# First norm of a decoder step: conditioning weights by quarters, 1/rms spread without a copy, last product's chunks in another order

## The chip, the cores and the metric

The kernel runs on one core of a Trainium2 chip. The metric is the device time of one execution in microseconds; below, "us" is always that. The engines are named as in the profile: PE (TensorE matmul), PEld (its weight loads), DVE (VectorE), ACT (ScalarE), POOL (GpSimd), SP (SyncE, which issues most DMAs).

## The reference, cut to what matters

One layer of a decoder works on 1024 prompt rows and 8 x 8 sample rows, 1088 rows of 1024 features. The prompt and each of the 8 sample sequences have a conditioning vector of their own, so there are 9 sets of shift and scale.

```
def rms_norm(x, g):
    y = xf * lax.rsqrt(jnp.mean(xf * xf, axis=-1, keepdims=True) + NORM_EPS)
    return y * g
def ada_mod(c, w, b):
    m = jax.nn.silu(c) @ w + b
    shift, scale, gate = jnp.split(m, 3, axis=-1)
...
h = rms_norm(x, norm_mix) * (1 + sc) + sh
P = h @ w_in                      # 1024 x 4352, in 34 blocks of 128 columns
... RWKV-7 branch, pooling branch, merge, w_out, residual
h = rms_norm(x, norm_mlp) * (1 + sc) + sh
x = x + gt * (square(relu(h @ w_ff1)) @ w_ff2)
y = rms_norm(x, norm_final)
```

## The kernel before, in words

Features lie on the 128 partitions and the 1088 rows along the free dimension, so x is eight tiles of 128x1088 (index kb). All large products are done in three passes with split operands: a value is split into hi (rounded) and lo (the rest), and each product is hi*hi + hi*lo + lo*hi (`mm3`, three matmuls). One row kb of h therefore becomes two tiles, `self.hh[kb]` and `self.hl[kb]`; in the profile both are called hx, and their numbers tell them apart (hx_147 and hx_148 are hi and lo of kb 0, hx_149 and hx_150 of kb 1, up to hx_161 and hx_162 of kb 7). A block of w_in is loaded in two halves of four kb each (`weights`, L157: a DMA to wraw, an ACT rounding to whi at L167, a DVE or POOL subtraction to wlo at L168). An output block has three chunks of columns (CH: 364, 362, 362), so one kb of one block takes 9 matmuls.

**Order of the work.** On DVE, ACT, POOL and SP a scheduler of the framework sets the order of the instructions; on PE the order is that in which the code emits them. `Pace` (L80) decides it: a counter `pace.t` adds an estimated time for each matmul, `back` is the stream of large products, and a `fore` generator yields the time to wait before its next step is put between them.

**The start** (`start`, L341, called in `phase1`). The eight x tiles are loaded by SP, squared on ACT (L361) and summed on DVE (L365). `smp` is the sample part of x, loaded once more in its own layout by a DMA on ACT's queue (L349). `stats` sums over the partitions with nine matmuls into po. `rms` (L281) takes the square root on ACT, the reciprocal on DVE (rt, 128x9), copies it to 128 columns for each of the nine blocks (R, L289), transposes these on PE (L155) so that 1/rms lies along the rows on all partitions, and copies the result from PSUM to rb on ACT (L302).

Shift and scale are made by `ada_part` (L239). w_ada_mix lies in thirds of 1024 columns, of which part 0 holds shift and scale of kb 0 to 3 and part 1 those of kb 4 to 7; eight DMAs of 512 KB load a part (aw, L371). A round of four small matmuls (32x512, wc<-aw,sT) multiplies two kb; four rounds make a part. ACT copies the sum to asb (L255), four matmuls with the table sel turn it into columns (L260; these are called the vector products below), DVE adds the bias (am, L263) and makes g = (1 + scale) * norm (L268). Then for each kb DVE makes h = x*g*rb (L390), ACT hi = round(h + shift) (L392), DVE lo = h + shift - hi (L394), and the 64 sample columns go by smp (L385 to L387, L393, L395).

The first two blocks of w_in, J4 and J12, are taken kb by kb in turn (`order` in `phase1`): 18 matmuls for each kb, 144 in all, and then the other 32 blocks of the stream, block by block. Part 0 of the conditioning stands before all of them, part 1 in the midst: `part(1, (0, 0, 3000, 1500), 1500)`.

**The end** (`phase2`: `last`, L1380, and `norm3`, L1401). The last group of the w_ff2 product goes by three chunks of columns, FCH = (0, 448), (448, 384), (832, 256); for each of the eight blocks m DVE adds the product to x (L1433; the 64 sample columns, which are the last ones, take an extra DVE step at L1436 and an addition on POOL, L1438), ACT squares it (L1410), DVE sums the squares (L1412), PE makes the stats, `rms` gives rb, and DVE multiplies (L1423; in the last chunk two blocks go by POOL and ACT, L1420 and L1421) before SP stores o_y (L1424). `rms` is also called in `norm2` (L1278), the norm before the second half of the layer.

Of the kernel before, what the change touches and what calls it, by code (L numbers as in the profile page):

```python
# [18 lines left out]
P = 128  # L19
# [98 lines left out]
class K:  # L118
# [162 lines left out]
    def rms(self, po, col, blocks, out, pool):  # L281
# [6 lines left out]
        R = self.row(pool, "R", 1, w=9 * 128).rearrange("p (b j) -> p b j", j=128)  # L288
        nc.vector.tensor_copy(R[:, :k, :], r.unsqueeze(2).to_broadcast([P, k, 128]))  # L289
        yield 2000  # L290
        for i in range(0, k, 4):
            m = min(4, k - i)
            ps = self.ps("wc")
            for j in range(m):
                self.tr(ps[:, j * 128:(j + 1) * 128], R[:, i + j, :], self.kc("ident"))
# [45 lines left out]
    def start(self, st, order):  # L341
# [4 lines left out]
        aw = lambda: st.tile([P, 1024], F32, tag="aw", bufs=8, name=self.nm("aw"))  # L346
        asb = st.tile([P, 512], F32, name="asb")
        smp = st.tile([P, 8, 64], F32, name="smp")
        nc.scalar.dma_start(smp, io["xT"][:, :, NPR:NT].rearrange("k p n -> p k n"))  # L349
# [6 lines left out]
        for kb in range(8):  # L356
            x = self.row(st, "x", 8)
            nc.sync.dma_start(x, io["xT"][kb])
            xs.append(x)
            sq = self.row(st, "sq", 3)  # L360
            nc.scalar.activation(sq, x, AF.Square)  # L361
            if t is None:
                t = sq
            else:
                nc.vector.tensor_tensor(t, t, sq, op=ALU.add)  # L365
        ws = []

        def load(i):
            for k in range(8):
                ws.append(aw())  # L370
                nc.sync.dma_start(ws[-1], io["w_ada_mix"][k, i])  # L371
# [3 lines left out]
        self.stats(po, t, blocks, True, True)  # L375
        rb = self.row(st, "rb", 1)
        pr, sa = slice(0, NPR), slice(NPR, NT)

        def part(i, gaps, turn):
            yield from self.ada_part("w_ada_mix", i, lambda: ws.pop(0), asb, self.am, "b_mix", (4 * i, 8 + 4 * i), gaps, turn)  # L380
            self.mod_scale(g, self.am, "norm_mix", 4 * i, 4 * i + 4)
            ks = slice(4 * i, 4 * i + 4)
            seq = lambda t: t[:, ks, 1:9].unsqueeze(3).to_broadcast([P, 4, 8, 8])
            s4 = smp[:, ks].rearrange("p k (q t) -> p k q t", t=TS)
            nc.vector.tensor_tensor(smp[:, ks], smp[:, ks], rb[:, sa].unsqueeze(1).to_broadcast([P, 4, 64]), op=ALU.mult)  # L385
            nc.vector.tensor_tensor(s4, s4, seq(g), op=ALU.mult)
            nc.vector.tensor_tensor(s4, s4, seq(self.am), op=ALU.add)  # L387
# [1169 lines left out]
```

## Time and profile before

| | us |
|---|---|
| three runs: median (lowest to highest) | 1761.83 (1758.38 to 1764.14) |
| the profiled execution, its own time | 1760.32 |
| its span in the trace | 1758.5 |
| PE busy in the span | 1688.9 (96%) |
| DVE busy / ACT busy / POOL busy | 846.8 / 546.0 / 242.9 |
| HBM read and written | 138.64 MB and 38.84 MB |

The profiled execution took 1.8 us more than its span, and 1.5 us less than the median. A row of a timeline gives the start in us from the span's start, the time until the end, the engine, the line, what is written and read, how many instructions of the kind are merged, and in brackets how long the engine had been idle and what ended that.

### The profile page before, as it was taken

What the parts mean: (1) busy time and instruction counts of PE and PEld (TensorE: products, weight loads), DVE (VectorE), ACT (ScalarE), POOL (GpSimd) and SP (SyncE); (2) the same over time, 40 slices, a digit from 0 to 9 for tenths busy, and PEclk for the clock granted to TensorE, in tenths of its full rate; (3) what the DMA queues carried; (4) which work ended last, traced back from release to release, by engine and by line L of the source; (5) the groups of instructions that cost most, each with busy time, mean ns of one, the idle gap of its engine ahead of it and who ended that gap; (6) DMA issues with size and microseconds to landing.
All of it is one profiled execution on the core that took longest, in us unless ns stands there. A gap on an engine that the chain in (4) does not pass through costs nothing.

```text
span 1758.5 us, 32538 instructions
## 1 busy us (share of the span) xinstructions
PE 1688.9 (96%) x13705; PEld 1582.7 (90%) x13705; DVE 846.8 (48%) x1546; ACT 546.0 (31%) x1100; POOL 242.9 (14%) x315
## 2 busy tenths in 40 slices
PE   5999999999999999998999999999999999999997
PEld 2989879887887898897889999999999999999996
DVE  5577475646663654344436643333333343323356
ACT  4443343334333433221224521213121222212132
POOL 0110111000000000003313511111111111111111
PEclk9999999999999999998999999999999999999999
DMA  8233314232413332849742211111111111111112
GB/s 336 83 126 119 124 65 138 83 104 88 131 42 127 97 120 72 315 156 356 257 150 78 85 61 42 49 43 43 48 42 48 44 43 48 42 49 43 43 42 103
DMA packets 80084, 179.61 MB, mean 102 GB/s; under 512 B 16481, under 2 KB 23137, under 8 KB 79937
## 3 DMA queue, kind: packets, MB, share of 16 engines
q1 hardware_dynamic: 72128, 156.66, 26.0%
q10 hardware_dynamic: 7664, 20.42, 3.4%
q8 instruction: 108, 1.77, 0.4%
q0 software_dynamic: 144, 0.44, 0.1%
q14 instruction: 40, 0.32, 0.1%
HBM read 138.64 MB, written 38.84 MB: 101 GB/s over the span
## 4 chain that ended last, share of the span: by engine, by line
PE 86%; DVE 5%; DMA 4%; ACT 2%; issue 1%; SPq 0%; DVEq 0%; ACTq 0%; POOL 0%
PE mm L148 58%; PE w L148 24%; PE wc L148 3%; DMA smp<-in_xT 1%; PE w L155 1%; DMA wt<-d_x 1%; DMA wraw<-in_w_in 1%; DVE wlo L168 1%; DMA d_th<-px 0%; DMA hx<-in_xT 0%; DMA t<-d_th 0%; DVE ma L1305 0%; DMA aw<-in_w_ada_mix 0%; DVE hx L1423 0%; DVE t L1303 0%
## 5 line engine op out<-in xcount | busy, mean ns | idle before, releaser
L148 PE MATMUL mm<-hx,whi 128*128 128x362 f32 (+2 forms) x2608 | 684.6, 344 | 9.0 <-DVE t L1246 6.5
L148 PEld LDWEIGHTS mm<-hx,whi 128*128 128x128 f32 x2608 | 459.0, 192 | 47.6 <-issue 28.4
L148 PE MATMUL mm<-hx,wlo 128*128 128x362 f32 (+3 forms) x1304 | 430.1, 330 | 1.8 <-DVE wlo L168 1.8
L167 ACT ACTIVATE whi<-wraw 128x512 fp32r<-128x512 f32 x246 | 155.0, 630 | 537.4 <-PE w L148 365.3
L148 PE MATMUL mm<-ma,whi 128*128 128x364 f32 (+1 forms) x1280 | 318.8, 330 | 0.0
L148 PEld LDWEIGHTS mm<-hx,wlo 128*128 128x128 f32 x1304 | 250.5, 192 | 2.3 <-DVE wlo L168 2.1
L148 PEld LDWEIGHTS mm<-ma,whi 128*128 128x128 f32 x1280 | 227.0, 189 | 6.7 <-issue 5.0
L168 DVE TENSOR_TENSOR wlo<-wraw,whi 128x512 fp32r<-128x512 f32 x157 | 111.9, 713 | 210.6 <-ACT whi L167 210.0
L148 PE MATMUL mm<-ma,wlo 128*128 128x364 f32 (+1 forms) x640 | 210.7, 329 | 0.0
L168 POOL TENSOR_TENSOR wlo<-wraw,whi 128x512 fp32r<-128x512 f32 x89 | 117.3, 1318 | 666.4 <-ACT whi L167 666.2
L1433 DVE SCALAR_TENSOR_TENSOR hx<-mm,aq,hx 128x364 f32<-128x364 f32 (+4 forms) x136 | 74.7, 587 | 206.4 <-PE mm L148 206.3
L148 PE MATMUL w<-mb,whi 128*128 128x362 f32 x640 | 159.0, 330 | 0.6 <-DVE rs L1436 0.6
L148 PEld LDWEIGHTS mm<-ma,wlo 128*128 128x128 f32 x640 | 120.9, 189 | 0.0
L148 PEld LDWEIGHTS w<-mb,whi 128*128 128x128 f32 x640 | 114.0, 191 | 0.8 <-issue 0.8
L1327 DVE TENSOR_TENSOR ft<-ft 128x362 f32<-128x362 f32 (+1 forms) x96 | 53.0, 576 | 127.4 <-ACT ft L1326 127.0
L148 PE MATMUL w<-mb,wlo 128*128 128x362 f32 x320 | 105.4, 329 | 1.3 <-DVE wlo L168 1.3
L148 PE MATMUL w<-hx,whi 128*128 128x362 f32 x416 | 103.5, 330 | 0.1
L148 PE MATMUL mm<-hid,whi 128*128 128x364 f32 (+4 forms) x304 | 75.3, 330 | 0.0
L148 PEld LDWEIGHTS w<-hx,whi 128*128 128x128 f32 x416 | 73.4, 190 | 1.2 <-issue 0.8
L1326 ACT ACTIVATE ft<-mm 128x364 f32<-128x364 f32 x64 | 29.3, 474 | 128.4 <-PE mm L148 128.3
L148 PE MATMUL w<-hx,wlo 128*128 128x362 f32 x208 | 67.8, 326 | 0.0
L148 PEld LDWEIGHTS w<-mb,wlo 128*128 128x128 f32 x320 | 61.1, 191 | 1.7 <-DVE wlo L168 1.7
(301 smaller groups left out, 2074.5 us busy)
## 6 DMA issues: line engine op xcount, KB each, us to landing
wraw<-in_w_ff SPq DMA_DIRECT2D x134, 256.0 KB, 2.6
wraw<-in_w_in SPq DMA_DIRECT2D x68, 256.0 KB, 3.0
hid<-in_w_ada_mlp SPq DMA_DIRECT2D x24, 512.0 KB, 5.1
d_th<-px SPq DMA_DIRECT2D x22, 544.0 KB, 3.1
wt<-d_x SPq DMA_DIRECT2D x20, 544.0 KB, 4.3
t<-d_th ACTq DMA_DIRECT2D x16, 544.0 KB, 6.7
aw<-in_w_ada_mix SPq DMA_DIRECT2D x16, 512.0 KB, 7.1
wraw<-in_w_out SPq DMA_DIRECT2D x32, 256.0 KB, 2.7
```

The source lines that it names most:

```text
L148: return self.nc.tensor.matmul(out, lhsT, rhs, **kw)
L155: self.nc.tensor.transpose(out, in_, ident)
L167: nc.scalar.activation(hi, raw, AF.Copy)
L168: (nc.gpsimd if n % 2 and n >= self.solo else nc.vector).tensor_tensor(lo, raw, hi.bitcast(F32), op=ALU.subtract)
L1326: nc.scalar.activation(t[:, :n], ps[:, :n], AF.Relu)
L1327: nc.vector.tensor_tensor(t[:, :n], t[:, :n], t[:, :n], op=ALU.mult)
L1433: nc.vector.scalar_tensor_tensor(x[:, c0:c0 + m], ps[:, :m], gt[:, 0:1], x[:, c0:c0 + m], op0=ALU.mult, op1=ALU.add)
```

## The change

**The conditioning by quarters.** w_ada_mix is no longer taken in two parts of 1024 columns but in four quarters (`qi`) of 512: shift and scale of two kb. A quarter is loaded by four DMAs of 512 KB (two tiles of 128x2x4x256, so pieces of 1 KB instead of 4 KB), and takes two rounds of four matmuls and one step of four vector products with 9 columns. The table for these is sel, summed once on POOL from the two halves of the old one. Quarter 0 is done before the large products begin, in a fixed order: round, stats, round, `rms`, asb, vector products, `rows(0)`. Quarters 1 to 3 stand among the products by `rest`: waits of 1000, 4500 and 5000 before a quarter's first round, 500 between its rounds, 1200 before its vector products, and none behind these.

**Two rows of h from each.** `rows(qi)` makes kb 2*qi and 2*qi + 1; for kb 0 and 1 h, hi and lo are made in three pieces, the chunks CH. The sample part is multiplied for two kb at a time.

**smp** is loaded by POOL instead of ACT. The last square and its addition are cut in two, 512 and 576 columns.

**1/rms without a copy.** R is gone: the transposes read rt with a stride of zero, in all calls of `rms`. In the first norm their results go to three tiles of the tag mm; in the last chunk of the kernel the six DVE multiplications read 1/rms from PSUM (`self.rps`).

**The last product.** FCH is turned round: the columns 640 to 1088 come first, with the samples, then 256 to 640, then 0 to 256. In the first chunk all eight m are multiplied in order; in the second m 0 to 3, and m 4 to 7 are written in the code behind the stats of the third.

```
-        R = self.row(pool, "R", 1, w=9 * 128).rearrange("p (b j) -> p b j", j=128)
-        nc.vector.tensor_copy(R[:, :k, :], r.unsqueeze(2).to_broadcast([P, k, 128]))
...
-                self.tr(ps[:, j * 128:(j + 1) * 128], R[:, i + j, :], self.kc("ident"))
+                self.tr(ps[:, j * 128:(j + 1) * 128], r[:, i + j:i + j + 1].to_broadcast([P, 128]), self.kc("ident"))
+            self.rps = ps
+            if out is None:
+                return
...
-        nc.scalar.dma_start(smp, io["xT"][:, :, NPR:NT].rearrange("k p n -> p k n"))
+        nc.gpsimd.dma_start(smp, io["xT"][:, :, NPR:NT].rearrange("k p n -> p k n"))
+        sel = st.tile([P, 9], F32, name="sel4")
+        nc.gpsimd.tensor_tensor(sel, self.kc("sel")[:, 0:9], self.kc("sel")[:, 9:18], op=ALU.add)
...
-        def load(i):
-            for k in range(8):
-                ws.append(aw())
-                nc.sync.dma_start(ws[-1], io["w_ada_mix"][k, i])
+        def load(qi):
+            for r in range(2):
+                w = st.tile([P, 2, 4, 256], F32, tag="aw", bufs=4, name=self.nm("aw"))
+                for s in range(2):
+                    o = s * 512 + qi % 2 * 256
+                    nc.sync.dma_start(w[:, s], io["w_ada_mix"][4 * r:4 * r + 4, qi // 2, :, o:o + 256].rearrange("k p c -> p k c"))
+                ws.append(w)
...
         load(0)
         back = self.stream(None, order)
-        self.stats(po, t, blocks, True, True)
+        load(1)
...
+        def round_(qi, r):
+            if r == 0:
+                ps[qi] = self.ps("wc")
+            w = ws.pop(0)
+            for k in range(4):
+                self.mm(ps[qi][32 * k:32 * k + 32, :], self.sT[:, 4 * r + k, :], w[:, :, k, :], start=r == 0, stop=r == 1, tile_position=(0, 32 * k))
+
+        def vectors(qi, wait):
+            kb = 2 * qi
+            asb = st.tile([P, 512], F32, tag="asb", bufs=1, name=self.nm("asb"))
+            nc.scalar.activation(asb, ps.pop(qi), AF.Copy)
+            yield wait
+            pv = self.ps("wc")
+            for i in range(4):
+                self.mm(pv[:, i * 9:(i + 1) * 9], asb[:, i * 128:(i + 1) * 128], sel, start=True, stop=True)
...
+            self.mod_scale(g, self.am, "norm_mix", kb, kb + 2)
...
+        def head():
+            round_(0, 0)
+            self.stats(po, t, blocks, True, True)
+            round_(0, 1)
+            yield from self.rms(po, 0, blocks, rb, "mm")
...
-        self.pace.run(iter(()), [part(0, (0, 3500, 0, 0), 1000), self.rms(po, 0, blocks, rb, st)])
-        load(1)
+        first()
+        rows(0)
+        load(2)
+        load(3)
...
-            yield from part(1, (0, 0, 3000, 1500), 1500)
+            for qi in range(1, 4):
+                yield (1000, 4500, 5000)[qi - 1]
+                round_(qi, 0)
+                yield 500
+                round_(qi, 1)
+                yield from vectors(qi, 1200)
+                rows(qi)
...
+                if ci == 2:
+                    for o in late:
+                        o()
+                yield from self.rms(po, 0, bl, rb[:, c0:c0 + n])
...
+                if ci < 2:
+                    late = [] if ci == 0 else [lambda m=m, out=out, r=rb[:, c0:c0 + n]: out(m, r) for m in range(4, 8)]
+                    for m in range(8 if ci == 0 else 4):
+                        out(m, rb[:, c0:c0 + n])
+                else:
+                    for m in (7, 6, 0, 1, 2, 3, 4, 5):
+                        out(m, rb[:, c0:c0 + n] if m > 5 else self.rps[:, :n], m > 5)
...
-FCH = [(0, 448), (448, 384), (832, 256)]
+FCH = [(640, 448), (256, 384), (0, 256)]
```

**Where instructions move: PE, the last vector products of the first norm.** Before, the vector products of part 1 (wc_410, from asb) make shift and scale of kb 4 to 7, whose first tile is hx_155; the rows around them are these:

```order
L148 MATMUL mm_373<-hx_149,wlo_243 128x362
L148 MATMUL wc_410<-kct,asb 128x18 x4
L148 MATMUL mm_356<-hx_151,whi_236 128x364
L148 MATMUL mm_356<-hx_152,whi_236 128x364
L148 MATMUL mm_356<-hx_151,wlo_237 128x364
```

Now the vector products of quarter 3 (wc_539, from asb_528) make shift and scale of kb 6 and 7, whose first tiles are hx_159 and hx_160:

```order
L148 MATMUL mm_355<-hx_157,wlo_488 128x362
L148 MATMUL wc_539<-sel_175,asb_528 128x9 x4
L148 MATMUL mm_333<-hx_159,whi_473 128x364
L148 MATMUL mm_333<-hx_160,whi_473 128x364
L148 MATMUL mm_333<-hx_159,wlo_474 128x364
```

Before, 36 matmuls of kb 2 and 3 stood between the vector products and the first matmul on a tile that they lead to; now there are none in quarter 3, 9 in quarter 2 (between wc_449 and hx_155) and 15 in quarter 1 (between wc_374 and hx_151).

**DVE, quarter 2.** Before, in part 1, DVE's rows from the vector products (am from wc_410) to the first lo tile (hx_156) were these:

```order
L263 TENSOR_TENSOR am<-wc_410,part 128x2x36
L268 SCALAR_TENSOR_TENSOR g_172<-am,part 128x36
L386 TENSOR_TENSOR smp<-smp,g_172 128x256
L390 SCALAR_TENSOR_TENSOR h_420<-x_198,g_172,rb_255 128x1024
L390 SCALAR_TENSOR_TENSOR h_426<-x_203,g_172,rb_255 128x1024
L387 TENSOR_TENSOR smp<-smp,am 128x256
L394 SCALAR_TENSOR_TENSOR hx_156<-h_420,am,hx_155 128x1024
```

Now the lo parts of the second half of the weights, wlo_474 and wlo_489, stand among them:

```order
L168 TENSOR_TENSOR wlo_474<-wraw_471,whi_473 128x512
L402 TENSOR_TENSOR am<-wc_449,part 128x2x18
L268 SCALAR_TENSOR_TENSOR g_172<-am,part 128x18
L413 SCALAR_TENSOR_TENSOR h_456<-x_199,g_172,rb_245 128x1024
L416 TENSOR_TENSOR smp<-smp,g_172 128x128
L413 SCALAR_TENSOR_TENSOR h_465<-x_204,g_172,rb_245 128x1024
L168 TENSOR_TENSOR wlo_489<-wraw_486,whi_488 128x512
L417 TENSOR_TENSOR smp<-smp,rb_245 128x128
L419 SCALAR_TENSOR_TENSOR hx_156<-h_456,am,hx_155 128x1024
```

In the other quarters the rows are the same without the two wlo; the kb 2, 4 and 6 have their lo tile behind both h of the quarter.

**ACT, before the square root of the first norm.** rt is the square root (w_176 and w_177 hold the stats), whi the rounded weights of J4 and J12. Before:

```order
L361 ACTIVATE sq_215<-x_213 128x1088
L286 ACT_TABLE_LOAD
L286 ACTIVATE rt_261<-w_176,eps 128x9
L302 ACTIVATE rb_255<-wc_266 128x512
L302 ACTIVATE rb_255<-wc_272 128x512
L167 ACTIVATE whi_236<-wraw_234 128x512
```

Now:

```order
L363 ACTIVATE sq_216<-x_214 128x576
L167 ACTIVATE whi_229<-wraw_227 128x512
L167 ACTIVATE whi_235<-wraw_233 128x512
L286 ACT_TABLE_LOAD
L286 ACTIVATE rt_264<-w_177,eps 128x9
L395 ACTIVATE asb_282<-wc_246 128x512
```

Both whi, which wait for their DMAs, have moved ahead of the table load and the square root; on DVE both wlo stand ahead of the reciprocal in the same way. On SP the two wraw are issued behind four DMAs of w_ada_mix instead of eight.

At the end of the kernel the eight multiplications of the second chunk (128x384) stand on DVE ahead of the last four additions of the third, in both kernels.

64 lines of the change are left out of this document (35 added, 29 removed).

## The prediction

> **What bounds the kernel now.** I read the chain that ended last, then windows by stage, then the timeline of the start and of the end. The chain by engine, three stages of the start, a stretch of the middle:
>
> ```profile
> PE 86%; DVE 5%; DMA 4%; ACT 2%; issue 1%; SPq 0%; DVEq 0%; ACTq 0%; POOL 0%
> 22.60:37.70 15.10, 13.25 (x66) 4.10 (x65) 8.07 (x13) 5.65 (x10) 0.00 (x0) 1.00 1.05 403
> 37.70:53.80 16.10, 16.03 (x100) 13.32 (x98) 12.90 (x19) 6.98 (x15) 0.00 (x0) 1.00 0.26 106
> 53.80:55.90 2.10, 0.27 (x3) 0.01 (x1) 2.10 (x5) 1.07 (x2) 0.00 (x0) 1.00 0.01 4
> 1000.00:1200.00 200.00, 200.00 (x1211) 200.00 (x1211) 75.95 (x137) 46.75 (x92) 34.04 (x37) 1.00 0.16 51
> ```
>
> (The columns of a window: us, then busy us and instructions of PE, PEld, DVE, ACT and POOL, granted clock, DMA share, GB/s.) PE is the bound: in the middle it is never idle, and a large matmul takes 200/1211 = 0.165 us. Whatever PE loses at the start moves all that follows; only the start and the end, where PE waits, can give anything. The start to the first rows of h:
>
> ```profile
> GB/s 0 58 211 410 409 410 411 425 405 401 403 417 421 239 0 237 361 353 291 324 397 415 430 419 417 397 306 348 419 433 415 395 424 419 415 433 401 69 0 0
> SPq L371 <- DMA smp<-in_xT: 10.3, 1, 10.3
> 17.24 1.28 ACT L286 ACT_TABLE_LOAD   x1
> 22.66 0.27 ACT L286 ACTIVATE rt<-w,eps 128x9 f32<-128x9 f32 x1 [4.14 <-PE w L148]
> 23.21 1.35 DVE L289 COPY R<-rt 128x1152 f32<-128x1152 f32 x1
> 24.62 1.12 PE L155 MATMUL wc<-kct,R 128*128 128x128 f32 x4
> 30.26 1.33 ACT L167 ACTIVATE whi<-wraw 128x512 fp32r<-128x512 f32 x2 [2.09 <-DMA wraw<-in_w_in]
> 34.07 2.47 DVE L390 SCALAR_TENSOR_TENSOR h<-x,g,rb 128x1024 f32<-128x1024 f32 x2
> 39.19 0.35 DVE L395 TENSOR_TENSOR hx<-smp,hx 128x64 fp32r<-128x64 f32 x2
> 39.46 0.19 PEld L148 LDWEIGHTS w<-hx,whi 128*128 128x128 f32 x1 [0.37 <-DVE hx L395]
> ```
>
> The DMAs run at about 410 GB/s (40 slices of 45 us) with a hole of 239, 0 and 237, some 2 us, while SP waits for smp before it issues aw. The first h begins at 34.07, and PE has the first block's third chunk, with the samples, at 39.46.
>
> **The change, the start: what comes earlier.** The hole goes, since SP no longer waits for smp (-2 us). wraw stands behind 2.1 MB of aw instead of 4.2: at 410 GB/s -5.1 us, so it lands at 30.26 - 7.1 = 23.2. The DMAs now move pieces of 1 KB; nothing here shows their price, so I take the rate as it is, and add up to 0.8 us in the range. But ACT now does both whi first (1.33: to 24.5), then the table load that was hidden under the stats before (1.28: 25.8), then the root (0.27: 26.1). Against 22.93 the root is 3 us later. Then the reciprocal (0.25 with its gaps), nine transposes of rt at 1.12/4 (2.5; R's 1.35 us are saved here; a source with stride zero costs, I assume, what R's cost), the vector products (0.96, row below) and am and g (0.5): h begins at about 30.3, and at 29 if PE is quicker by half at the transposes.
>
> The steps from there on, each with its row:
>
> ```profile
> 41.46 1.06 PE L148 MATMUL wc<-aw,sT 128*32 128x512 f32 x8
> 46.73 0.96 PE L148 MATMUL wc<-kct,asb 128*128 128x18 f32 x8
> 47.54 0.57 PE L148 MATMUL mm<-hx,whi 128*128 128x364 f32 x2
> 47.73 0.23 DVE L263 TENSOR_TENSOR am<-wc,part 128x72 f32<-128x72 f32 x1 [3.13 <-PE wc L148]
> 48.00 0.20 DVE L268 SCALAR_TENSOR_TENSOR g<-am,part 128x36 f32<-128x36 f32 x1
> 48.23 0.42 DVE L386 TENSOR_TENSOR smp<-smp,g 128x256 f32<-128x256 f32 x1
> 48.57 2.47 DVE L390 SCALAR_TENSOR_TENSOR h<-x,g,rb 128x1024 f32<-128x1024 f32 x2
> 51.29 2.48 DVE L394 SCALAR_TENSOR_TENSOR hx<-h,am,hx 128x1024 fp32r<-128x1024 f32 x2
> 1722.01 4.85 DVE L1423 SCALAR_TENSOR_TENSOR hx<-hx,part,t 128x448 f32<-128x448 f32 x8
> 1740.11 4.33 DVE L1423 SCALAR_TENSOR_TENSOR hx<-hx,part,t 128x384 f32<-128x384 f32 x8
> ```
>
> For kb 0 and 1 DVE works in pieces: from 4.85/8 = 0.61 for 448 columns and 4.33/8 = 0.54 for 384, a piece of 364 takes 0.52 and one of 298 0.45. Its order has six pieces of h (2.98), a smp step (estimated at 0.29 for half of 256 columns), then lo: the first after 3.8 us; five more pieces of lo, two smp steps and the sample columns: another 3.2. So PE has the chunk with the samples at 30.3 + 7.0 = 37.3, against 39.46: 2.2 us earlier.
>
> **What PE then still has to do.** Until the next block begins it has 137 matmuls in both kernels (22.6 us). Before, two rounds and one step of vector products were left; now six rounds and three steps. That is 4 x 1.06 + 2 x 0.81 (46.73 to 47.54) = 5.9 us more, work that before lay in the waits of the first 37 us. Without any stall PE would reach the next block at 37.3 + 22.6 + 6 x 1.06 + 3 x 0.81 + 0.5 of small gaps = 69.2. Before it was there at 69.13 (row below), stalls included (39.5 + 22.6 + 2 x 1.06 + 0.81 + 0.5 and 3.5 for the stall below and the slow clock after it make 69.0): so far nothing is won.
>
> **The stalls that it adds.** From the end of a quarter's vector products to its first lo tile DVE needs, by the rows above, 51.29 + 1.24 - 47.73 = 4.8 us, and 4.5 with smp half as wide. PE needs that lo with its second matmul. As the order in front shows, PE's cover between is 15 matmuls in quarter 1, 9 in quarter 2, none in quarter 3 (36 before, 5.9 us, which is why this stall is not in the trace now).
> - Quarter 1: 4.5 - 16 x 0.165 = 1.9.
> - Quarter 2: wlo_474 stands ahead of am and waits for whi, which waits for PE's last use of the old weights right before the vector products: 0.63 + 0.69 + 0.1 - 0.81 = 0.6 later; wlo_489 adds 0.7. So 5.8 - 10 x 0.165 = 4.1.
> - Quarter 3: 4.5 - 0.165 = 4.3.
> - In each the chunk with the samples waits again: smp, the second lo and hx<-smp stand behind the first lo, 0.29 + 1.24 + 0.2 = 1.7, and PE comes to it after five matmuls, 0.8: 0.9 each, 2.7.
>
> Together 13.0 us. Then the clock. Before, PE has one such stall, and this followed it:
>
> ```profile
> 55.16 1.28 DVE L168 TENSOR_TENSOR wlo<-wraw,whi 128x512 fp32r<-128x512 f32 x2
> 55.90 0.43 PE L148 MATMUL mm<-hx,wlo 128*128 128x364 f32 x1 [1.83 <-DVE wlo L168]
> 57.00:58.00 1.00, 1.00 (x5) 1.00 (x5) 1.00 (x3) 0.33 (x1) 0.00 (x0) 0.50 0.84 256
> 58.00:59.00 1.00, 1.00 (x5) 1.00 (x4) 1.00 (x2) 0.82 (x1) 0.00 (x0) 0.50 0.67 250
> 60.00:61.00 1.00, 1.00 (x6) 1.00 (x6) 0.30 (x1) 0.00 (x0) 0.59 (x1) 0.84 0.09 16
> 61.00:62.00 1.00, 1.00 (x8) 1.00 (x7) 0.00 (x0) 0.00 (x0) 1.00 (x3) 1.00 0.21 62
> 69.13 0.50 PE L148 MATMUL mm<-hx,whi 128*128 128x364 f32 x2
> ```
>
> After 1.83 us of waiting PE ran at half clock for about 3.4 us, which costs 1.7. I take one such spell for each of the three stalls, 5.1, less the 0.8 of each sample wait that slow matmuls cover: +2.7. The Trainium skill ("TensorE: Matmul & The Clock Gate", What's actually happening) has the clock halve after an idle window of about 3.4 us and return after as long a busy one. The trace agrees with the return, but its drop came after 1.83; by the page quarter 1 would keep its clock, and the sum would be 0.9 lower.
>
> So PE begins the next block at 69.2 + 13.0 + 2.7 = 84.9, against 69.13: **+15.8 us**. The old stall of 1.83 and its spell are in the 69.13.
>
> **The middle.** In norm2 and in the first two chunks of the end PE's place for the transposes is fixed and R is ready before it comes there; leaving R out is worth nothing. POOL's sel and smp are hidden: smp is used only after 30 us.
>
> **The end.** The rows of the last chunk:
>
> ```profile
> 1748.07 1.05 PE L148 MATMUL wc<-kct,t 128*128 128x2 f32 x8 [2.87 <-DVE t L1412]
> 1749.65 0.29 DVE L289 COPY R<-rt 128x256 f32<-128x256 f32 x1
> 1750.09 0.66 PE L155 MATMUL wc<-kct,R 128*128 128x128 f32 x2 [0.97 <-DVE R L289]
> 1750.79 0.38 ACT L302 ACTIVATE t<-wc 128x256 f32<-128x256 f32 x1 [1.37 <-PE wc L155]
> 1751.20 3.40 DVE L1423 SCALAR_TENSOR_TENSOR hx<-hx,part,t 128x256 f32<-128x256 f32 x6 [1.26 <-ACT t L302]
> ```
>
> The eight multiplications of 4.33 us still stand ahead of the last additions, so `late` moves nothing. The samples leave the last chunk: four steps rs and a POOL addition go, about 0.4. R goes (0.44 with its gap), and rb on the way to six of the eight multiplications (0.41); the two on POOL and ACT still wait for it, and reading PSUM may cost 0.06 each (0.4). I take **-1.1 us**, from -0.3 to -1.8.
>
> **The sum.** 15.8 - 1.1 = +14.7 us. The profiled execution took 1760.32, so this one would take 1775.0; the median of the runs lies 1.5 above it: **1776.5 us**.
>
> **The rivals.**
> 1. Half the loss: the start gains 2 us more (quick transposes, pieces of 1 KB free) and the clock drops at most once. Then 15.8 - 2 - 3 - 1.1 = +9.7: 1771.5. Against it: three stalls in place of one, two of them twice as long.
> 2. More: the clock stays at half through two spells after each stall, and in the first chunk of kb 0, since PE idles much between 28 and 37. Each further spell costs 1.7, so up to +6: 1782.
> 3. Not slower: the delay is taken back later. Between 69 and 800 PE waits for ACT and DVE in the recurrent branch:
>
> ```profile
> PE w L148 <- ACT wt L577: 5.6, 8, 1.2
> PE w L148 <- DVE wt L1018: 3.7, 3, 2.8
> 200.00:400.00 200.00, 192.42 (x2307) 170.23 (x2308) 116.22 (x221) 75.99 (x168) 15.33 (x31) 0.98 0.28 94
> ```
>
> If these engines ran behind on work of their own, 15 us of head start would let these waits go: without these 9.3 the time is 1767, and with the smaller ones of their kind it falls to 1762 or below. It decides once more than 9 us have vanished. Against it: each of these chains starts from a product that PE itself has just made, and from 200 to 400 DVE is busy for 58% of the time and ACT for 38%, so they follow PE, late as it is.
> 4. SP's hole stays. The Trainium skill ("DMA: Bandwidth & Descriptors", Issuing engines are not separate DMA queues) says that another issuing engine saves only the sequencer's time. The waits row above is a wait for a semaphore, which does go; if it stayed, wraw would land 2 us later: 1778.5, within the range.
>
> **How the numbers follow.** Forecast 0.70, rival 1 0.10, rival 2 0.10, rival 3 0.06, rival 4 0.04. The range reaches from rival 1, less the uncertain end and the shares of the stalls (1768), to rival 2 (1783). A measurement of this kernel tells about 0.3%, 5.3 us, from no change. Rival 3 gives 0.06: half of it faster (0.03), the other within 0.3%, where I put 0.02 of rival 1's lower tail too (0.05). The rest is slower (0.92).
>
> **What would show it.** In the profile of the changed kernel: the root of the first norm at 26 instead of 22.7, behind two whi; h from about 30; then PE waiting for DVE's lo tiles three times, near 2, 4 and 4.5 us, right behind the vector products, with a clock of 0.5 after them; the next block's first matmul near 85 instead of 69; the end some 1 us shorter from PE's last product. If that block begins by 72, or if PE's waits between 85 and 815 are more than 9 us smaller than before, I am wrong.

## The result, and the profile after

The changed kernel takes 1786.97 us (median of 4 runs, 1783.54 to 1788.89), the kernel before 1762.99 beside it (4 runs, 1758.38 to 1771.96): a ratio of 1.0123, 95% interval 1.0100 to 1.0147 (the quotient of the two medians is 1.0136, inside it). It is slower, as forecast, but by 24 us where 14.7 were forecast, and outside the range. The profiled execution took 1786.41 us, with a span of 1784.6; that is 26.1 more than before's span. Medians here are of fast executions: one of 5703.76 us of the kernel before (experiments 9 to 11) and one of 6937.32 us in the eighth experiment are left out.

The start of the changed kernel, from the timelines of PE, ACT and DVE in order of time: the conditioning round, the stats, the second round, the transposes and the vector products on PE; both whi, the table load and the root on ACT; the first piece of h on DVE; and the first block's third chunk.

```profile
19.25 1.94 PE L148 MATMUL wc<-aw,sT 128*32 128x512 f32 x8 [19.25 <-DMA aw<-in_w_ada_mix]
21.12 4.00 PE L148 MATMUL w<-kct,sq 128*128 128x9 f32 x18
25.05 1.93 PE L148 MATMUL wc<-aw,sT 128*32 128x512 f32 x8
26.91 2.18 PE L155 MATMUL mm<-kct,rt 128*128 128x128 f32 x9
28.89 1.72 PE L148 MATMUL wc<-sel,asb 128*128 128x9 f32 x8
...
22.82 1.34 ACT L167 ACTIVATE whi<-wraw 128x512 fp32r<-128x512 f32 x2 [5.42 <-DMA wraw<-in_w_in]
24.17 1.28 ACT L286 ACT_TABLE_LOAD   x1
25.46 0.27 ACT L286 ACTIVATE rt<-w,eps 128x9 f32<-128x9 f32 x1
...
31.16 1.54 DVE L413 SCALAR_TENSOR_TENSOR h<-x,g,rb 128x364 f32<-128x364 f32 x3
...
38.01 0.97 PE L148 MATMUL w<-hx,whi 128*128 128x362 f32 x2 [1.21 <-ACT hx L420]
```

The weights, the root and h come within 0.9 us of the forecast (the weights on time although the DMAs moved 355 GB/s from 15 to 27 us, where the forecast took 410). But the five PE rows join without a gap: PE is busy from 19.25 to 30.6, and all of it at half speed, since a round of 1.94 takes 1.06 later on.

The next rows are PE's waits in quarters 1 to 3, each behind its vector products, and the first matmul of the next block:

```profile
45.45 0.95 PE L148 MATMUL wc<-sel,asb 128*128 128x9 f32 x8
49.41 0.43 PE L148 MATMUL mm<-hx,whi 128*128 128x364 f32 x1 [0.42 <-ACT hx L414]
51.02 0.44 PE L148 MATMUL mm<-hx,whi 128*128 128x364 f32 x1 [1.18 <-DVE hx L419]
52.55 0.43 PE L148 MATMUL w<-hx,whi 128*128 128x362 f32 x1 [0.27 <-DVE hx L421]
58.35 0.95 PE L148 MATMUL wc<-sel,asb 128*128 128x9 f32 x8
62.62 0.43 PE L148 MATMUL mm<-hx,whi 128*128 128x364 f32 x1 [1.73 <-ACT hx L414]
64.83 0.67 PE L148 MATMUL mm<-hx,whi 128*128 128x364 f32 x1 [1.78 <-DVE hx L419]
75.80 0.95 PE L148 MATMUL wc<-sel,asb 128*128 128x9 f32 x8
79.75 0.44 PE L148 MATMUL mm<-hx,whi 128*128 128x364 f32 x1 [3.00 <-ACT hx L414]
81.37 0.67 PE L148 MATMUL mm<-hx,whi 128*128 128x364 f32 x1 [1.18 <-DVE hx L419]
88.64 0.50 PE L148 MATMUL mm<-hx,whi 128*128 128x364 f32 x2
```

The three stalls are there: idle 1.9, 3.5 and 4.2 us, 9.6 in all. The next block begins at 88.64, against 69.13 before (+19.5) and 84.9 forecast. The slow clock took more than forecast. These rows are two windows of the changed kernel with a granted clock of 0.50, and then, from its timeline, two conditioning rounds (8 passes; at full speed 1.06):

```profile
64.00:70.00 6.00, 5.17 (x17) 5.17 (x18) 2.45 (x5) 0.40 (x2) 0.00 (x0) 0.50 0.12 44
81.00:84.00 3.00, 2.63 (x9) 2.63 (x10) 1.99 (x5) 0.50 (x3) 0.82 (x1) 0.50 0.00 0
```

```profile
39.21 1.94 PE L148 MATMUL wc<-aw,sT 128*32 128x512 f32 x8
42.29 1.63 PE L148 MATMUL wc<-aw,sT 128*32 128x512 f32 x8
```

The rounds show that PE still runs at half speed at 39 to 43, although the column of the granted clock says 1.00 there: the trace holds no report of the throttle before 43.5, and without one the column reads 1.00. The length of a known instruction is the surer sign.

A further 6.9 us are lost where nothing was forecast. From the next block's first matmul to the first of the layer's second half the windows are, of the kernel before and then of the changed one:

```profile
69.13:931.70 862.57, 832.73 (x8566) 742.12 (x8565) 467.39 (x870) 302.68 (x641) 86.25 (x122) 0.98 0.41 140
```

```profile
88.64:958.10 869.46, 834.91 (x8566) 743.30 (x8565) 473.61 (x870) 302.34 (x641) 86.82 (x122) 0.98 0.41 139
```

The same 8566 passes take 6.9 us longer: 2.2 more busy, 4.7 more idle. PE's longest waits in that stretch, before and after:

```profile
PE mm L148 <- DVE t L1246: 6.5, 1, 6.5
...
PE w L148 <- issue: 4.1, 3, 1.9
```

```profile
PE mm L148 <- DVE t L1292: 7.7, 1, 7.7
PE w L148 <- issue: 6.9, 4, 2.6
```

"Issue" is a wait for nothing that the profile shows. Its three large ones in the changed kernel stand in bursts of small matmuls (32x32, 382 instructions on PE within some 2 us, four bursts in the kernel):

```profile
215.45 0.21 PE L148 MATMUL w<-hv,iv 32*32 32x32 f32 x1 [1.88 <-issue]
376.50 0.69 PE L148 MATMUL w<-hv,iv 32*32 32x32 f32 x32 [2.62 <-issue]
707.60 0.59 PE L148 MATMUL w<-hv,iv 32*32 32x32 f32 x25 [2.25 <-issue]
```

The kernel before has two, of 1.93 and 1.68, in the second and the fourth burst, and none in the first.

The end, with the rows that answer to those of before:

```profile
1774.09 1.87 PE L148 MATMUL wc<-kct,t 128*128 128x2 f32 x8 [2.57 <-DVE t L1458]
1776.60 0.66 PE L155 MATMUL wc<-kct,rt 128*128 128x128 f32 x2 [0.64 <-DVE rt L287]
1777.71 2.44 DVE L1473 SCALAR_TENSOR_TENSOR hx<-hx,part,wc 128x256 f32<-128x256 f32 x6 [1.26 <-ACT t L303]
```

From PE's last product to the end of the span it takes 13.1 us (1784.6 - 1774.09 + 2.57), before 13.25. What the samples and R save is there, but the stats fell into slow clock (1.87 instead of 1.05). rb saves nothing: the last row still waits for ACT's copy of 1/rms (t, L303), although it reads the result in PSUM (wc).

### The profile page after: what moved, and what is told of

Its sections match the earlier page's. It is cut to its first block, busy times and chain, and to the rows that moved or that the text cites. A ratio compares the mean times of both kernels' runs of the same rounds, so it can differ in the third digit from the quotient of the medians.

```text
span 1784.6 us, 32609 instructions
## 1 busy us (share of the span) xinstructions
PE 1699.3 (95%) x13721; PEld 1589.3 (89%) x13721; DVE 850.8 (48%) x1559; ACT 549.1 (31%) x1107; POOL 243.7 (14%) x317
## 3 DMA queue, kind: packets, MB, share of 16 engines
q1 hardware_dynamic: 78272, 156.66, 26.1%
## 4 chain that ended last, share of the span: by engine, by line
PE 86%; DVE 5%; ACT 2%; DMA 2%; issue 1%; POOL 0%; DVEq 0%; SPq 0%; ACTq 0%; POOLq 0%
PE mm L148 58%; PE w L148 24%; PE wc L148 4%; PE w L155 1%; DMA hx<-in_xT 1%; DMA wt<-d_x 1%; DVE wlo L168 0%; DMA t<-d_th 0%; DVE ma L1351 0%; DVE hx L1473 0%; DVE t L1349 0%; DVE h L413 0%; ACT whi L167 0%; DVE bk L657 0%; DVE t L1338 0%
## 5 line engine op out<-in xcount | busy, mean ns | idle before, releaser
L148 PE MATMUL mm<-hx,whi 128*128 128x362 f32 (+2 forms) x2608 | 687.4, 345 | 23.1 <-DVE t L1292 7.7
L1492 DVE SCALAR_TENSOR_TENSOR hx<-mm,aq,hx 128x364 f32<-128x364 f32 (+3 forms) x136 | 74.7, 587 | 205.7 <-PE mm L148 205.7
L1375 DVE TENSOR_TENSOR hx<-ft,hx 128x362 fp32r<-128x362 f32 (+1 forms) x66 | 51.4, 800 | 23.7 <-ACT hx L1374 23.5
```

The lines of the kernel that those rows point to most:

```text
L148: return self.nc.tensor.matmul(out, lhsT, rhs, **kw)
L1375: nc.vector.tensor_tensor(lo[:, c0:c0 + n], t[:, :n], hi[:, c0:c0 + n].bitcast(F32), op=ALU.subtract)
L1492: nc.vector.scalar_tensor_tensor(x[:, c0:c0 + m], ps[:, :m], gt[:, 0:1], x[:, c0:c0 + m], op0=ALU.mult, op1=ALU.add)
```

## The experiments

All times of the kernel before are of the same call and chip. "Next block" is the first matmul of the third block of w_in, 69.13 before and 88.64 in the changed kernel.

### 1. The end alone

The function `start` of the kernel before, all else of the change:

```
-        first()
-        rows(0)
...
+        self.pace.run(iter(()), [part(0, (0, 3500, 0, 0), 1000), self.rms(po, 0, blocks, rb)])
```

> The first norm of the kernel before (two parts, smp on ACT's queue, its order of PE) with everything else of the change: 1/rms spread without a copy, the last product's chunks turned round. Theory A (the whole loss arises before PE's next block of w_in, and the 6.8 us that appear between that block and the end of the merge follow from the late start): the next block's first matmul near 69 us as before, the middle unchanged, the end 0.3 to 1.8 us shorter, so 0.9990 to 0.9998 of the kernel before, about 1762 us. Rival B (the spreading without a copy or the turned chunks carry part of the loss, for instance the 6.8 us of the middle): 3 to 7 us slower than before, 1766 to 1770.

Measured: 1760.23 us against 1762.42, ratio 0.9989 (0.9978 to 1.0001). The next block begins at 67.85; the stretch behind it is 864.4 long, as against 862.6 before and 869.5 in the changed kernel:

```profile
67.84:932.20 864.36, 835.34 (x8566) 744.61 (x8565) 470.02 (x870) 302.94 (x641) 86.62 (x122) 0.97 0.41 140
```

So the spreading without a copy and the turned chunks cost nothing that can be measured, and the loss belongs to the new first norm: theory A.

### 2. More matmuls between vector products and rows

```
-                yield (1000, 4500, 5000)[qi - 1]
+                yield (0, 2000, 4000)[qi - 1]
...
-                yield 500
+                yield 200
...
-                yield from vectors(qi, 1200)
+                yield from vectors(qi, 600)
```

> The changed kernel with one table of numbers changed: waits of 0, 2000 and 4000 before the quarters' first rounds, 200 between the rounds, 600 before the vector products, so that 30, 45 and 48 large matmuls stand between a quarter's vector products and its first rows of h, instead of 15, 9 and 0. Theory A (the stalls come from too few matmuls between): the PE waits of quarters 1 to 3 (9.6 us in the trace, 10.9 with the refilling behind each) go, and the 4.5 us of half clock behind them; the kernel before's own stall behind the new weights (1.8 us and 1.7 of slow clock) comes back; two rounds fall into PE's wait for the first h, 2 us: 12 to 15 us less than the changed kernel, 1772 to 1775. Rival B (DVE or the weights' transfers are the limit, so PE waits elsewhere in the same place, for aw or for lo): less than 5 us gained, 1782 or more.

Measured: 1770.39, ratio 1.0043 (1.0026 to 1.0059), 16.6 us less than the changed kernel. Of its PE waits between 30 and 75 us two are left, that for the first rows of h and the kernel before's own wait for wlo; below them, from the timeline, the next block:

```profile
PE mm L148 <- DVE hx L419: 1.8, 1, 1.8
PE mm L148 <- DVE wlo L168: 1.4, 1, 1.4
```

```profile
73.90 0.49 PE L148 MATMUL mm<-hx,whi 128*128 128x364 f32 x2
```

Theory A: all three stalls go with three lines of waits changed, and 14.7 of the 19.5 us with them. Not all of that is cover: two rounds now also fill the waits of 1.9 and 1.2 us that PE had for the first rows of h. The stretch behind stays long, 869.0: that loss is another one.

### 3. Root first

```
-        nc.scalar.activation(hi, raw, AF.Copy)
...
+                nc.scalar.activation(hi, raw, AF.Identity, bias=bias[0])
...
         nc.vector.reciprocal(r, r)
...
+            nc.vector.tensor_scalar(zb, r[:, 0:1], 0.0, None, op0=ALU.mult)
...
+            self.stats(po, t, blocks, True, True)
             round_(0, 0)
-            self.stats(po, t, blocks, True, True)
```

The bias of the first two whi is zb, a zero made from the reciprocal, so both wait for it.

> The changed kernel with the square root of the first norm ahead of both whi on ACT and the reciprocal ahead of both wlo on DVE (the rounding of the weights is tied to the reciprocal by a zero made from it), and the stats ahead of both rounds on PE. Theory A, the prediction's step (the root is late because ACT rounds both weights first): root at 23, h from 28, and the kernel 3 us faster than the changed one, 1784. Rival B (from 19.3 to 30.6 PE is busy without a break at half speed with round, stats, round, transposes, vector products, 11.8 us, and this sets h): root at 23.3 but the transposes and h come at most 0.6 us earlier, and the time stays within 1 us of the changed kernel's 1787.

Measured: 1786.83, ratio 1.0132 (1.0114 to 1.0151). The root, PE's rounds and transposes behind it, and h:

```profile
23.05 0.27 ACT L296 ACTIVATE rt<-w,eps 128x9 f32<-128x9 f32 x1 [3.75 <-PE w L149]
...
22.94 3.64 PE L149 MATMUL wc<-aw,sT 128*32 128x512 f32 x16
26.51 2.15 PE L156 MATMUL mm<-kct,rt 128*128 128x128 f32 x9
...
30.01 1.54 DVE L428 SCALAR_TENSOR_TENSOR h<-x,g,rb 128x364 f32<-128x364 f32 x3
```

The root comes 2.4 us earlier, h only 1.15, the time is that of the changed kernel (+24.4 us against the kernel before, which had +24.0): nearer to rival B. ACT's queue was not what set h; PE was.

### 4. PE kept awake

```
+            for _ in range(n):
+                nc.tensor.matmul(pw[:, :128], wz, wz, start=True, stop=True)
...
+            warm(74)
...
+            warm(8)
```

> The changed kernel with 74 matmuls of zeros (128x128, nothing reads them) on PE from 1 us on, while it otherwise waits until 19.25 for the first weights, and 8 more behind the first vector products. Theory A (PE starts slow after standing idle, and stays so until 43.5): round, stats, transposes and vector products take about half of their 11.8 us, h begins 1.5 to 2 us earlier (the root still waits for both whi), and the products between 38 and 43.5 run at full speed, 2.7 us: together 4 to 5 us, 1782 to 1783. Rival B (these matmuls are slow for another reason, their operands or the transfers beside them): round 1.9, stats 4.0 and transposes 2.2 us as now, 1787.

Measured: 1786.06, ratio 1.0138 (1.0118 to 1.0157). PE's rows at the start:

```profile
1.06 18.28 PE L429 MATMUL mm<-wz 128*128 128x128 f32 x148 [1.06 <-DVE wz L424]
20.64 1.06 PE L148 MATMUL wc<-aw,sT 128*32 128x512 f32 x8 [1.30 <-DMA aw<-in_w_ada_mix]
21.64 2.17 PE L148 MATMUL w<-kct,sq 128*128 128x9 f32 x18
```

The mechanism is A's: the same round takes 1.06 instead of 1.94, the stats 2.17 instead of 4.00, and h begins at 28.97. Then the clock falls again, the transposes take 2.18 as before, and the rounds at 37 and 40 us are slow once more (1.94, 1.86). The next block is 1.8 us earlier, and the median shows no gain. The stretch behind it is 871.2 long, more than the changed kernel's 869.5.

### 5 and 6. The place of the bursts

Counted in the traces (a weight load and a matmul for each pass, and each separate wait), every one of the full stalls put down to issue, in all 14 traces, stands where the number of PE instructions ahead of it leaves 193 when divided by 256 (the expectations count one on in places: 193 or 194): 3009, 6593 and 14017 in the changed kernel, 6593 and 14017 before. A burst of 382 crosses one or two such numbers, and it is at the second that PE stands; only in the last burst of the fourth experiment, where the first lies 6 instructions behind the burst's start, did the second cost no more than 0.58 us. Two experiments shift the stream by matmuls of zeros while PE has nothing to do, 36 in the changed kernel and 11 in the kernel before:

```
+        for _ in range(36):
+            nc.tensor.matmul(pw[:, :128], wz[:, :128], wz[:, :128], start=True, stop=True)
```

> The changed kernel with 36 matmuls of zeros (128x128, nothing reads them) on PE in its first 11 us, when it has nothing to do: 145 PE instructions more ahead of everything else, and PE idle again long before the first weights land. Counting PE's instructions in the traces (two for each pass of a matmul, one for each separate wait), all stalls of about 2 us put down to issue so far stand at a number that leaves 193 or 194 when divided by 256, in bursts of 382 small instructions. Theory A (the stall comes where such a burst crosses its second multiple, so the number of instructions ahead decides): of the changed kernel's three stalls (behind w<-hv,iv near 215, 376 and 707) all three go and one comes near 540; PE's waits put down to issue fall from 6.9 us to about 2, and the time by 4 to 5 us, to 1782. Rival B (the stalls come from transfers or from the late start): they stay where they are, 1787.

> The kernel before with 11 such matmuls of zeros in PE's first 4 us, 45 instructions more, which puts its bursts where the changed kernel has them. Theory A (the place in the instruction stream): a third stall of about 2 us appears behind the first burst, near 193, and those near 353 and 683 stay; waits put down to issue rise from 4.1 to 6.5 or more, the time by 2 us. Rival B (the third stall of the changed kernel comes with its late start or its new order of work): two stalls as before, 4.1 us.

The kernel before, shifted by 44 instructions in the trace: its third stall, from the timeline, and the window from the next block on.

```profile
195.59 0.25 PE L148 MATMUL w<-hv,iv 32*32 32x32 f32 x3 [1.80 <-issue]
```

```profile
69.03:941.90 872.87, 839.18 (x8567) 747.94 (x8566) 469.27 (x870) 303.16 (x641) 86.58 (x122) 0.97 0.40 139
```

It has the third stall at the place foretold, 6.8 us put down to issue instead of 4.1, and its stretch is 10.3 us longer than before's, with the same start. Its time is 1766.79 against 1763.42, ratio 1.0019 (1.0004 to 1.0033). Of the 10.3 us, 6.4 are longer busy time for the same passes and 3.9 are idle, and the traced execution, 1770.47, is 3.7 above the median: what the time shows is 3.4 us. So a third stall and a longer middle need neither a late start nor the quarters: 11 matmuls of zeros at the head of the kernel before bring them. These also wake PE, from 1.2 to 5.9 us; the median alone can't tell that from the shift.

The changed kernel, shifted by 145: the only full stall, in the third burst, where there was none.

```profile
537.68 0.81 PE L148 MATMUL w<-hv,iv 32*32 32x32 f32 x38 [2.09 <-issue]
```

Waits put down to issue fall to 3.9 (two waits of about 1 us appear at first crossings), and the stretch is 864.8 long instead of 869.5. But the median is 1790.99 (1784.72 to 1793.18), ratio 1.0147 (1.0126 to 1.0169): place as in A, no gain in time. The profiled execution was the shortest of the five.

### 7 and 8. Put together

The first experiment's kernel with 46 such matmuls (128x176), and the changed kernel with the edits of the second and third and 36 matmuls (128x232).

> The kernel of the first experiment (old first norm, the rest of the change) with 46 matmuls of zeros, 128x176, on PE from 1 us to about 18, 185 instructions. Theory A (clock after standing idle, and place of the bursts): stats in 2.2 us instead of 4.0, the first norm's root 1.8 us earlier and with it h and the next block by 1 to 2 us, as far as the weights' transfers let them; one burst stalls instead of two, 2 us; together 2 to 4 us less than the first experiment, 1756 to 1758, 0.9965 to 0.998 of the kernel before. Rival B (the first rows of h wait for the weights' transfers, and the stalls for something else): as the first experiment, 1760.

> The changed kernel with all that helped: more matmuls between a quarter's vector products and its rows (the second experiment), root ahead of both whi and stats ahead of the rounds (the third), and 36 matmuls of zeros, 128x232, from 1 us to about 18. Theory A (stalls for lack of cover, PE at half speed at the start, and the bursts' place explain the loss): against the second experiment's 1770.4 the rows of h come 3 to 4 us earlier, the products up to 44 run at full speed (2 us) and one burst stalls in place of three (4 us): 1761 to 1765, the same as the kernel before. Rival B (a part of the loss is still unknown, in the middle): 1767 or more.

The seventh takes 1766.35, ratio 1.0012 (0.9997 to 1.0026): its next block is at 67.82 as in the first, so waking PE gains nothing there, and it is 5 us slower than the first experiment, each set against its own kernel before (+2.9 and -2.2), against both theories. The eighth takes 1766.81, ratio 1.0026 (1.0008 to 1.0044): its next block is at 71.06, only 1.9 us behind the kernel before, but the time is 1.8 us more than A allowed for, and just short of B.

### 9. A control that failed

64 matmuls of 128x64 in the place of the 36 of the fifth, 257 instructions.

> The control to the fifth experiment: the changed kernel with 64 matmuls of zeros, 128x64, in PE's first 11 us. They keep PE awake as long as there, but make 257 instructions, so the bursts stay where the changed kernel has them, but for one. Theory A (the place of the bursts is worth its 3 us, and waking PE early costs something that hid it): stalls near 215, 376 and 707 again, waits put down to issue near 6.9 us, and a median 3 us or more above the fifth experiment's 1791, 1794. Rival B (the stalls' place does not show in the time): the stalls are back, the median stays within 1.5 us of 1791. Rival C (waking PE early costs nothing): 1787.

```profile
1.20 27.57 PE L381 MATMUL mm<-wz 128*128 128x64 f32 x128 [1.20 <-DVE wz L378]
```

These narrower matmuls never brought PE to full speed: from one pass to the next it takes 0.213 us throughout, while the 128 columns of the fifth take 0.213 at first and 0.111 from 7.5 us on. So they ran into the first round, everything began 9.1 us later (next block 97.73), and it is no control. It shows something else: the median is 1795.81, 8.8 above the changed kernel's (8.6, each set against its own kernel before). A delay of 9.1 at the start is paid nearly in full 1700 us later. The stalls are back in the first, second and fourth burst.

### 10. The kernel before without cover

```
-            yield from part(1, (0, 0, 3000, 1500), 1500)
+            yield from part(1, (0, 0, 3000, 1500), 7600)
```

> The kernel before with one number changed: its vector products of part 1 wait 7600 instead of 1500 behind the rounds, so that no large matmul stands between them and the first row of h that needs them, instead of 36. Theory A (cover decides): PE waits there for the chain of am, g, h, hi and lo, 4.6 us for lo and its hi before it, and the stall behind the new weights (1.8 us) falls into this wait: 3 to 5 us more at the next block with the samples' wait and the slow clock, 1766 to 1768. Rival B (DVE and ACT get ahead some other way, or PE's waits come from elsewhere): within 1.5 us of the kernel before.

```profile
53.69 0.96 PE L148 MATMUL wc<-kct,asb 128*128 128x18 f32 x8
58.34 0.44 PE L148 MATMUL mm<-hx,whi 128*128 128x364 f32 x1 [3.69 <-ACT hx L392]
59.88 0.67 PE L148 MATMUL mm<-hx,whi 128*128 128x364 f32 x1 [1.11 <-DVE hx L394]
74.42 0.49 PE L148 MATMUL mm<-hx,whi 128*128 128x364 f32 x2
```

The stall of the changed kernel's last quarter, made in the kernel before by one number: 4.8 us of waiting, half clock behind it (0.67 instead of 0.44), and the next block 5.3 us later. The time is 1765.58 against 1763.26, ratio 1.0017 (1.0004 to 1.0031), a little less than A said: of the 5.3 us only 2.3 are found in the median.

### 11. One part of the new start alone

The first experiment with smp loaded by POOL:

```
-        nc.scalar.dma_start(smp, io["xT"][:, :, NPR:NT].rearrange("k p n -> p k n"))
+        nc.gpsimd.dma_start(smp, io["xT"][:, :, NPR:NT].rearrange("k p n -> p k n"))
```

> The kernel of the first experiment with one part of the start's change put back: smp is loaded by POOL instead of ACT. Theory A (the transfers bound the old first norm, and SP's wait for smp leaves them a hole of 2 us): the hole goes, the last weights and h come 1 to 2 us earlier, the next block near 66 to 67 instead of 67.8, 1758 to 1759, the fastest of all. Rival B (PE at half speed, from the stats on, bounds the old first norm too): the next block near 67.8, 1760.

```profile
66.00 0.49 PE L148 MATMUL mm<-hx,whi 128*128 128x364 f32 x2
...
1750.51 1.05 PE L148 MATMUL wc<-kct,t 128*128 128x2 f32 x8 [2.56 <-DVE t L1413]
```

The next block is the earliest of all, 66.00, as A said. But A's 1758 to 1759 did not come: the time is 1762.97 against 1763.26, ratio 0.9994 (0.9981 to 1.0008), not to be told from the first experiment. Here the last stats ran at full speed, and from PE's last product to the end it took 12.05 us (1760.0 - 1750.51 + 2.56), 1.2 less than before. That is not the rule: in the 11 traces with the new end the last stats ran at full speed in three (1.05, here and in the eighth and twelfth experiments) and took 1.57 to 1.87 in the others, while in the three with the old end they always took 1.05.

### 12. The shift once more, without waking PE

36 matmuls of zeros, 32x32, behind the first vector products, where PE waits anyway.

> The changed kernel with 36 matmuls of zeros, 32x32, behind the first vector products, where PE waits 1.8 us for the first rows of h: 144 PE instructions more, but PE isn't woken early as in the fifth experiment. Theory A (the place of the bursts in the instruction stream makes the 7 us that the changed kernel loses between its next block and the second half of the layer): one full stall near 540 instead of three, that stretch 864 to 866 us long instead of 869.5, the start unchanged (next block 88.6), the median 4 to 5 us below the changed kernel's 1787. Rival B (shorter in the trace, but what the stalls cost is made up by PE's clock elsewhere): stalls as in A, the median within 1.5 us of 1787 or above.

```profile
534.89 0.79 PE L148 MATMUL w<-hv,iv 32*32 32x32 f32 x38 [2.06 <-issue]
```

```profile
87.51:952.30 864.79, 832.25 (x8566) 741.42 (x8565) 469.83 (x870) 302.36 (x641) 90.45 (x122) 0.98 0.41 140
```

The middle of the trace does what A said, 864.8 and one full stall (the next block, at 87.52, is 1.1 earlier than forecast), and the profiled execution is the shortest of four, 1781.55. The median is 1786.06 (ratio 1.0137, 1.0117 to 1.0157), as B said.

## Where the prediction was right and where it was wrong

Right: the direction; the hole that goes and wraw at 23 (22.8); the root at 26 (25.7); h at 30.3 (31.2); the third chunk at 37.3 (38.0); three stalls behind the vector products, because PE's cover was cut. That the cover is the cause of the stalls is shown from both sides, by the second and the tenth experiment. Rival 3, the delay taken back later, is out for the changed kernel: the ninth experiment's 9.1 us stay. In the kernel before, the tenth's 5.3 us shrink to 2.3 in the median; why stays open.

**"The root 3 us later because ACT does both whi first"**: the time was right, the weight laid on it wrong. In the changed kernel the stats end at 25.1, 2.5 us later than before, because a round at half speed stands ahead of them; freeing the root (third experiment) brings nothing in the time. What set h was 11.8 us of PE work at half speed: with the first round and the stats at full speed (fourth experiment) h began 2.2 us earlier.

**"Together 13.0 us" of stalls**: 9.6 us idle. Counted from one matmul's start to the next, with the refilling behind each wait, it is 10.9. The waits for the samples were 0.27 instead of 2.7.

**"+2.7" for the clock**, the step that failed first. It counted one spell of 3.4 us for each stall and none ahead. There was none behind quarter 1; but 6.8 us lie behind quarter 2 and 3.4 behind quarter 3, and PE had not yet come to full speed at 38, where the forecast had it there; it came to it near 43.5. PE's busy time in these three is 5.5 + 6.0 + 3.0 = 14.5 us, half of it lost: 7.3. With 0.7 from the third chunk, -2.1 from the stalls and +4.6 from the clock the 84.9 become 88.1; measured 88.64. Rival 2 named the slow first chunk and second spells like that behind quarter 2; it had a chance of 0.10.

**"The middle: worth nothing"**, the step that failed most: 6.9 us in the trace. The argument looked at what waits for what, and by that nothing changes. But 41 more PE instructions ahead shift the bursts to where three of them stand still instead of two, 2.8 us; PE's wait for t grows by 1.2 (it was 6.4 again in the twelfth experiment); the rest is small waits and slow clock. The sixth experiment makes this stretch long in the kernel before, the fifth and twelfth make it short in the changed one. Over all traces it is 868.9 to 872.9 long in the five with three full stalls, and 862.4 to 866.5 in the others but for one: the fourth experiment has two full stalls and 871.2, so the number of stalls is not the whole of it. The Trainium skill ("Runtime: NRT & Kernel Launch", Instruction fetch mechanics) says that instructions come in blocks of 256, and that crossing a block's end costs little and is mostly hidden. The traces agree with the 256, not with the price: 1.5 to 2.6 us for a full stall at the second crossing of a burst. That it is the fetching that is late was not measured by itself.

**"-1.1 us" for the end**: -1.2 in the eleventh experiment, where the last stats ran at full speed; -0.1 in the changed kernel's trace, where they didn't. The first is near by luck. The terms named add up to -0.85 (0.4, 0.44 and 0.41 saved, 0.4 lost), not -1.1. Measured in the eleventh experiment, the samples save 0.31 and R 0.33, near the forecast; rb saves nothing, as DVE still starts behind ACT's copy; and reading PSUM costs nothing, 0.47 us a multiplication, as four of the six took before. What made up for it was not forecast: the transposes ran faster (0.40 instead of 0.66), and the multiplications and stores took 0.33 less.

The sum of the trace: 19.5 + 6.9 - 0.1 for the layer's second half - 0.1 for the end = 26.2, against 26.1 of span.

How far this holds for the medians is shown by setting each kernel's start beside its time (us; kernel before 0):

| kernel | next block | median | difference |
|---|---|---|---|
| stream not shifted: 1, 10, 11 | -1.3, +5.3, -3.1 | -2.2, +2.3, -0.3 | -0.9, -3.0, +2.8 |
| changed kernel | +19.5 | +24.0 | +4.5 |
| three full stalls: 2, 3, 6, 9 | +4.8, +18.2, -0.1, +28.6 | +8.0, +24.4, +3.4, +32.6 | +3.2, +6.2, +3.5, +4.0 |
| one or two: 4, 5, 7, 8, 12 | +17.7, +19.9, -1.3, +1.9, +18.4 | +23.6, +27.6, +2.9, +3.4, +23.1 | +5.9, +7.7, +4.2, +1.5, +4.7 |

Every kernel whose PE stream was shifted loses 1.5 to 7.7 us more than its start explains, 4.5 on average; the three others lie around nothing (-3.0 to +2.8, -0.4 on average). The two ranges overlap, so one kernel alone decides little. And fewer full stalls do not make it less. So it is shown that the place of PE's instructions decides where the full stalls stand, and that shifted kernels are slower on the whole. That the shift itself makes them slower is not shown: the sixth and seventh also wake PE early, and the others have the new start too. Why the median does not follow the number of stalls stays open. One traced execution of each is too little for it, as executions of one kernel lie up to some 10 us apart (1759.63 to 1771.21 in the seventh experiment).

No version beats the kernel before by more than can be measured; the first experiment comes nearest (0.9989).

## What to carry to other kernels

When a change cuts a piece of preparation into smaller ones, count for each how much work of the bound engine stands between its last input and its first use, and compare it with the chain of the other engines: here 15, 9 and 0 matmuls against 4.5 to 5.8 us, and three lines of waits in the order of work gave back two thirds of the loss. Price a start on an engine that has stood idle at its slow speed, by the length of known instructions and not by the granted clock's column. And a change of a few tenths of a per cent may have to do with where instruction bursts fall in the stream (11 matmuls that nothing reads made 0.2% here); before arguing from such a difference, shift the stream of the kernel before and see.

## What the runs showed of the hardware

- Full stalls of 1.5 to 2.6 us in bursts of 382 small PE instructions, always behind a number of PE instructions that leaves 193 when divided by 256, in all 14 traces, movable by adding matmuls that nothing reads.
- Matmuls of 128x64 (f32), back to back for 27.6 us, left PE at half speed (0.213 us a pass); 128x128 brought it to full (0.111) after 6.3 us of the fifth experiment. The Trainium skill ("TensorE: Matmul & The Clock Gate", What's actually happening) has the clock rise after about 3.4 us of sustained work; by this trace not every sustained work counts.
- Kept awake, PE fell to half speed again at 24.7 while it was busy with stats, rounds and transposes, the only gap being 1.3 us ahead of them (fourth experiment). In the changed kernel 1.9 us of waiting in quarter 1 left the clock alone, 3.5 in quarter 2 cost 6.8 us of half clock, 4.2 in quarter 3 cost 3.4.
